# A row softmax on one Trainium2 core: the fourth chunk's load is split into rows 0 to 13 and rows 14 and 15

## The chip, the cores and the metric

The kernel runs on one core of a Trainium2 chip. The metric is the device time of one execution in microseconds (us), the median of several runs. One execution was also taken by the hardware profiler; all rows below come from it.

## The reference

```python
x: (16, 1024, 512) float32
x_scaled = x / 0.5
x_max = np.max(x_scaled, axis=-1, keepdims=True)
exp_x = np.exp(x_scaled - x_max)
out = exp_x / np.sum(exp_x, axis=-1, keepdims=True)
```

It is a softmax with temperature 0.5 over each of 16384 rows of 512 floats. 33.55 MB are read and 33.55 MB written.

## The kernel before

The 16384 rows are cut into 8 chunks (`C`), numbered from 0. A chunk gives each of the 128 partitions (`P`) 16 rows (`G`) that lie side by side in HBM, so one partition's share of a chunk is 32 KB in one piece, and a chunk is 4096 KB. Six buffers (`BUFS`) hold chunks; chunk 6 takes the buffer of chunk 0, and chunk 7 that of chunk 1, so their loads wait until those chunks have been stored.

**Loads.** `LOADS` lists, for each chunk, the row ranges that are loaded by a DMA each. Chunk 0 comes in two (rows 0 to 3, then 4 to 15), chunks 1 to 6 whole, chunk 7 without its last two rows (`LATE`). `load(c, queue)` issues them at L75. Chunk 0 goes on SyncE's queue. Chunks 1 and 3 go on ScalarE's queue at the very beginning; chunk 1 first waits until the first rows of chunk 0 have landed. The others are issued on SyncE's queue: 2, 4 and 5 at once, 6 after the store of chunk 0, 7 after the store of chunk 1. The last two rows of chunk 7 come on GpSimd's queue (`load_last_rows`, L111), in packets of 4 KB, after ScalarE has reached row 10 of chunk 5.

**Compute.** `BLOCKS` cuts the chunks into 11 blocks: chunk 0 into three, chunk 7 into two, the others whole. `shift(i)` finds a block's row maxima on VectorE (L92) and the bias of the exponential (L96). `exponentials` runs one instruction per row on ScalarE (L122), which also sums the row. `scale_vector` takes the reciprocal (L143) and multiplies most rows on VectorE (L145); `scale_scalar` multiplies the last few on ScalarE (L156). Everything works in place in the chunk's buffer. Only `shift` reads what a load has just brought: the maxima of a whole chunk wait for all of the chunk's DMAs.

**Stores.** Each chunk is stored whole, by one DMA on ScalarE's queue (L166), after its last block is scaled. So the queue of ScalarE carries, in this order, the loads of chunks 1 and 3 and then the eight stores. ScalarE issues them in the order of its own instructions.

**Order.** The schedule is written by hand (`tc.manual_schedule()`). The loop runs the exponentials of block i + 1, the scaling of block i, the maxima of block i + 2 and the store of block i. VectorE's order is therefore: scale a chunk, then the maxima two blocks on.

Of the kernel before, what the change touches and what calls it, by code (L numbers as in the profile page):

```python
# [1 line left out]

# [4 lines left out]


@with_exitstack
def kernel(  # L10
    ctx: ExitStack,
    tc: tile.TileContext,
    x: bass.AP,
    out: bass.AP,
):
    nc = tc.nc
    fp32 = mybir.dt.float32
    P = nc.NUM_PARTITIONS
    AX = mybir.AxisListType.X
    EXP = mybir.ActivationFunctionType.Exp  # L20
    COPY = mybir.ActivationFunctionType.Copy
    MAX = mybir.AluOpType.max

    D = x.shape[-1]
    xf = x.flatten_outer_dims()
    of = out.flatten_outer_dims()
    N = xf.shape[0]

    G = 16
    C = N // (P * G)
    assert C * P * G == N
    xr = xf.rearrange("(c p g) d -> c p g d", p=P, g=G)
    outr = of.rearrange("(c p g) d -> c p g d", p=P, g=G)
    WHOLE = [(0, G)]
    LATE = 2
    LOADS = [[(0, 4), (4, G)]] + [WHOLE] * 6 + [[(0, G - LATE)]]
    BLOCKS = [[(0, 4), (4, 8), (8, G)]] + [WHOLE] * 6 + [[(0, 8), (8, G)]]  # L40
    STORES = [WHOLE] * 8
    BMAX = 16
    BUFS = 6

    data = ctx.enter_context(tc.tile_pool(name="data", bufs=BUFS))
    stats = ctx.enter_context(tc.tile_pool(name="stats", bufs=6))

    ctx.enter_context(tc.manual_schedule())


    warm = stats.tile([P, 1], fp32, name="warm", bufs=1)
    nc.vector.memset(warm, 0.0)  # L52
    nc.scalar.activation(out=warm, in_=warm, func=EXP)  # L53

    chunks = {}
    blocks = [(c, lo, hi) for c in range(C) for lo, hi in BLOCKS[c]]
    n = len(blocks)
    biases, sums, recips = {}, {}, {}

    finished = []  # L60
    data_wait = mybir.DependencyInfo(
        mybir.DependencyClass.Sync, mybir.DependencyReason.DATA
    )
    for c in range(BUFS):
        chunks[c] = data.tile([P, G, D], fp32, name="xt")

    loaded = set()

    def load(c, queue):
        loaded.add(c)  # L70
        if c >= BUFS:
            chunks[c] = chunks[c - BUFS]
        xt = chunks[c]
        for lo, hi in LOADS[c]:
            part = queue.dma_start(out=xt[:, lo:hi, :], in_=xr[c][:, lo:hi, :])  # L75
            if c == 1:
                tc.add_manual_dep(
                    part.ins, finished[0], data_wait, reason="first rows come alone"
                )
            finished.append(part.ins.name)  # L80

    load(0, nc.sync)
    for c in (1, 3):
        load(c, nc.scalar)

    def shift(i):
        c, lo, hi = blocks[i]
        if c not in loaded:
            load(c, nc.sync)
        b = hi - lo  # L90
        negmax = stats.tile([P, BMAX], fp32, name="negmax")
        nc.vector.tensor_reduce(  # L92
            negmax[:, 0:b], chunks[c][:, lo:hi, :], axis=AX, op=MAX, negate=True
        )
        biases[i] = stats.tile([P, BMAX], fp32, name="bias")
        nc.vector.tensor_scalar_mul(biases[i][:, 0:b], negmax[:, 0:b], 2.0)  # L96

    def load_last_rows(signal):
        seen = stats.tile([P, 1], fp32, name="seen", bufs=1)
        copied = nc.gpsimd.tensor_copy(out=seen, in_=signal)  # L105
        finished.append(copied.ins.name)
        c = C - 1
        to = chunks[c - BUFS][:, G - LATE : G, :]
        of_ = xr[c][:, G - LATE : G, :]
        for p0, p1 in ((P - 2, P), (0, P - 2)):  # L110
            part = nc.gpsimd.dma_start(  # L111
                out=to[p0:p1], in_=of_[p0:p1], max_dma_last_dim=4 * D
            )
            finished.append(part.ins.name)

    def exponentials(i, rows):
        c, lo, hi = blocks[i]
        if i not in sums:
            sums[i] = stats.tile([P, BMAX], fp32, name="sums")
        for g in rows:  # L120
            row = chunks[c][:, lo + g, :]
            nc.scalar.activation(  # L122
                out=row,
                in_=row,
                func=EXP,
                bias=biases[i][:, g : g + 1],
                scale=2.0,
                accum_out=sums[i][:, g : g + 1],
            )
            if c == BUFS - 1 and g == 10:  # L130
                load_last_rows(sums[i][:, g : g + 1])


    def scalar_rows(i):
        c, lo, hi = blocks[i]
        return 4 if hi - lo == G else (hi - lo) // 8

    def scale_vector(i):
        c, lo, hi = blocks[i]
        b = hi - lo  # L140
        k = b - scalar_rows(i)
        recips[i] = stats.tile([P, BMAX], fp32, name="recip")
        nc.vector.reciprocal(recips[i][:, 0:b], sums[i][:, 0:b])  # L143
        rows = chunks[c][:, lo : lo + k, :]
        last = nc.vector.tensor_mul(  # L145
            rows, rows, recips[i][:, 0:k].unsqueeze(2).broadcast_to((P, k, D))
        )
        if i == n - 1:
            finished.append(last.ins.name)

    def scale_scalar(i):
        c, lo, hi = blocks[i]
        b = hi - lo
        for g in range(b - scalar_rows(i), b):
            row = chunks[c][:, lo + g, :]
            last = nc.scalar.activation(  # L156
                out=row, in_=row, func=COPY, scale=recips[i][:, g : g + 1]
            )
            if i == n - 1:
                finished.append(last.ins.name)  # L160

    def store(i):
        c, _, end = blocks[i]
        for lo, hi in STORES[c]:
            if hi == end:
                part = nc.scalar.dma_start(  # L166
                    out=outr[c][:, lo:hi, :], in_=chunks[c][:, lo:hi, :]
                )
                if c < C - 1:
                    finished.append(part.ins.name)  # L170

    shift(0)
    shift(1)

    def rows(i):
        c, lo, hi = blocks[i]
        cut = 6 if c == 1 else hi - lo
        return range(cut), range(cut, hi - lo)

    exponentials(0, rows(0)[0])  # L180
    for i in range(n):
        if i + 1 < n:
            exponentials(i + 1, rows(i + 1)[0])
        scale_vector(i)
        scale_scalar(i)
        if i + 2 < n:
            shift(i + 2)
        store(i)
        if i + 1 < n:
            exponentials(i + 1, rows(i + 1)[1])  # L190

    seen = nc.sync.nop()
    info = mybir.DependencyInfo(
        mybir.DependencyClass.Sync, mybir.DependencyReason.DATA
    )
    for name in finished:
        tc.add_manual_dep(seen.ins, name, info, reason="leaves one wait for the end")


# [1 line left out]
_INS = ['x']  # L201
_OUTS = [((16, 1024, 512), 'float32')]


# [23 lines left out]
```

## Time and profile before

| | |
|---|---|
| median of 3 runs | 161.92 us (161.68 to 162.12) |
| the profiled execution's own time | 161.71 us |
| its span, first to last instruction | 159.9 us |
| VectorE (DVE) busy | 128.3 us, 80% of the span |
| ScalarE (ACT) busy | 109.6 us, 69% of the span |
| bytes moved by DMA | 67.13 MB, 420 GB/s over the span |
| 4096 KB stores on ScalarE's queue | 8, median 20.9 us from issue to landing |

How to read it: the span leaves out some 1.8 us around the first and the last instruction. Busy time is counted for compute instructions alone; an instruction that issues a DMA or waits is not busy time. The lines of the page's second part cut the span into 40 slices of 4 us; the digit is the busy share in tenths. The 16 DMA engines of the core serve all queues; q10 in the profile is ScalarE's queue, q1 SyncE's and q0 GpSimd's. A packet is one contiguous piece, here one partition's share of a DMA, and is counted where it starts.

### The profile page before, as it was taken

The page shows a single profiled execution, that of the slowest core. Times are in us where ns is not written, and L with a number is a line of the kernel's source. Part 1 is how long each engine was busy: PE and PEld are TensorE (multiplying, and loading weights), DVE is VectorE, ACT ScalarE, POOL GpSimd, SP SyncE. Part 2 cuts the span into 40 slices and gives each one's busy share as a digit, 9 for nine tenths or more (in the row PEclk, how much of TensorE's full clock was granted, in tenths as well). Part 3 has the DMA queues.
Part 4 walks back from the last instruction along what each step waited for, and adds up shares of the span by engine and source line. Part 5 has one row for each costly group of instructions (what it writes and reads, how often), then busy time and mean ns, then how long its engine had stood idle before and what let it go on. Part 6 is the DMA issues. An engine that isn't in the chain of part 4 may idle for free.

```text
span 159.9 us, 422 instructions
## 1 busy us (share of the span) xinstructions
DVE 128.3 (80%) x45; ACT 109.6 (69%) x285; POOL 1.9 (1%) x7
## 2 busy tenths in 40 slices
DVE  0600599999999999999999999999999999955000
ACT  3070072924899999599959995999699899980000
POOL 0000000000000000000000000040000000000000
DMA  5999999999999999999999989898999999999994
GB/s 189 467 459 459 393 393 508 410 393 467 451 320 461 402 402 508 402 393 484 434 393 443 467 380 492 370 483 384 415 454 436 416 516 393 393 475 443 393 443 205
DMA packets 2642, 67.13 MB, mean 420 GB/s; under 512 B 336, under 2 KB 336, under 8 KB 464
## 3 DMA queue, kind: packets, MB, share of 16 engines
q10 hardware_dynamic: 1440, 41.94, 60.8%
q1 hardware_dynamic: 1008, 24.64, 36.5%
q0 software_dynamic: 192, 0.52, 0.8%
q14 instruction: 2, 0.02, 0.0%
HBM read 33.55 MB, written 33.55 MB: 420 GB/s over the span
## 4 chain that ended last, share of the span: by engine, by line
DVE 66%; ACT 10%; DMA 10%; issue 4%; SPq 0%
DVE negmax L92 39%; DVE xt L145 25%; ACT xt L122 10%; DMA xt<-in_x_dram 10%; DVE recip L143 1%; DVE bias L96 1%; SPq L75 0%
## 5 line engine op out<-in xcount | busy, mean ns | idle before, releaser
L122 ACT ACTIVATE xt<-xt,bias 128x512 f32<-128x512 f32 x128 | 90.4, 708 | 32.9 <-DVE bias L96 31.6
L92 DVE TENSOR_REDUCE negmax<-xt 128x16 f32<-128x8192 f32 (+2 forms) x11 | 69.9, 6353 | 14.2 <-DMA xt<-in_x_dram 14.2
L145 DVE TENSOR_TENSOR xt<-xt,recip 128x6144 f32<-128x6144 f32 (+2 forms) x11 | 55.6, 5056 | 0.4
L122 ACT ACTIVATION_READ_ACCUMULATOR xt<-xt,bias 128x1 f32 x128 | 23.9, 187 | 0.0
L156 ACT ACTIVATE xt<-xt,recip 128x512 f32<-128x512 f32 x27 | 17.3, 706 | 0.0
L143 DVE RECIPROCAL recip<-sums 128x16 f32<-128x16 f32 (+2 forms) x11 | 2.4, 220 | 2.1 <-ACT xt L122 2.1
L96 DVE TENSOR_SCALAR bias<-negmax 128x16 f32<-128x16 f32 (+2 forms) x11 | 1.9, 173 | 0.4
L53 ACT ACT_TABLE_LOAD x1 | 1.3, 1283 | 0.7 <-PEq L212 0.7
L111 POOL DMA_DIRECT2D xt<-in_x_dram x2 | 1.5, 744 | 0.5 <-issue 0.5
L105 POOL COPY seen<-sums 128x1 f32<-128x1 f32 x1 | 0.2, 186 | 105.2 <-ACT xt L122 105.2
L52 DVE MEMSET warm<- 128x1 f32 x1 | 0.1, 59 | 0.8 <-PEq L212 0.8
L53 ACT ACTIVATE warm<-warm 128x1 f32<-128x1 f32 x1 | 0.2, 203 | 0.0
L212 POOL MEMSET const-bfloat16-1.0<- 128x1 bf16 x1 | 0.1, 96 | 0.0
L212 POOL MEMSET const-uint8-127<- 128x1 uint8 x1 | 0.1, 96 | 0.0
L212 POOL MEMSET const-float32-0.0<- 128x1 f32 x1 | 0.1, 93 | 0.2 <-issue 0.2
L212 POOL MEMSET const-float32-1.0<- 128x1 f32 x1 | 0.1, 93 | 0.0
## 6 DMA issues: line engine op xcount, KB each, us to landing
out_dram<-xt ACTq DMA_DIRECT2D x8, 4096.0 KB, 20.9
xt<-in_x_dram SPq DMA_DIRECT2D x4, 4096.0 KB, 45.3
xt<-in_x_dram ACTq DMA_DIRECT2D x2, 4096.0 KB, 31.4
xt<-in_x_dram SPq DMA_DIRECT2D x1, 3584.0 KB, 25.3
xt<-in_x_dram SPq DMA_DIRECT2D x1, 3072.0 KB, 16.4
xt<-in_x_dram SPq DMA_DIRECT2D x1, 1024.0 KB, 4.7
xt<-in_x_dram POOLq DMA_DIRECT2D x1, 504.0 KB, 19.2
xt<-in_x_dram POOLq DMA_DIRECT2D x1, 8.0 KB, 8.6
```

What stands on the lines that cost most here:

```text
L52: nc.vector.memset(warm, 0.0)
L53: nc.scalar.activation(out=warm, in_=warm, func=EXP)
L92: nc.vector.tensor_reduce(negmax[:, 0:b], chunks[c][:, lo:hi, :], axis=AX, op=MAX, negate=True)
L96: nc.vector.tensor_scalar_mul(biases[i][:, 0:b], negmax[:, 0:b], 2.0)
L105: copied = nc.gpsimd.tensor_copy(out=seen, in_=signal)
L111: part = nc.gpsimd.dma_start(out=to[p0:p1], in_=of_[p0:p1], max_dma_last_dim=4 * D)
L122: nc.scalar.activation(out=row, in_=row, func=EXP, bias=biases[i][:, g : g + 1], scale=2.0, accum_out=sums[i][:, g : g + 1],)
L143: nc.vector.reciprocal(recips[i][:, 0:b], sums[i][:, 0:b])
L145: last = nc.vector.tensor_mul(rows, rows, recips[i][:, 0:k].unsqueeze(2).broadcast_to((P, k, D)))
L156: last = nc.scalar.activation(out=row, in_=row, func=COPY, scale=recips[i][:, g : g + 1])
L212: nc = _bacc.Bacc("TRN2", target_bir_lowering=False, num_devices=1)
```

## The change

`LOADS` gets a cut in its fourth entry, chunk 3. Its rows 0 to 13 of every partition (28 KB) are loaded by one DMA, and rows 14 and 15 (4 KB) by a second, both on ScalarE's queue, one behind the other, in the place where the one DMA of 32 KB per partition stood. Nothing else is edited: the same loop in `load` issues them, and the maxima of chunk 3 read both parts.

```diff
     WHOLE = [(0, G)]
     LATE = 2
-    LOADS = [[(0, 4), (4, G)]] + [WHOLE] * 6 + [[(0, G - LATE)]]
+    TAIL = 2
+    LOADS = [[(0, 4), (4, G)]] + [WHOLE] * 2 + [[(0, G - TAIL), (G - TAIL, G)]] + [WHOLE] * 3 + [[(0, G - LATE)]]
     BLOCKS = [[(0, 4), (4, 8), (8, G)]] + [WHOLE] * 6 + [[(0, 8), (8, G)]]
```

## The prediction

> **What bounds the kernel now.** I read the page first: VectorE is busy 80% of the span and ScalarE 69%, and the chain of waits puts two thirds of the span on VectorE, so VectorE looks like the bound. The page's slices of the DMA engines say otherwise:
>
> ```profile
> DMA  5999999999999999999999989898999999999994
> GB/s 189 467 459 459 393 393 508 410 393 467 451 320 461 402 402 508 402 393 484 434 393 443 467 380 492 370 483 384 415 454 436 416 516 393 393 475 443 393 443 205
> ...
> q10 hardware_dynamic: 1440, 41.94, 60.8%
> q1 hardware_dynamic: 1008, 24.64, 36.5%
> q0 software_dynamic: 192, 0.52, 0.8%
> ```
>
> The 16 DMA engines are full from the second slice to the last but one. q10 carries 41.94 MB, which is what ScalarE's queue issues (two loads and eight stores of 4096 KB); q1 carries SyncE's loads, q0 GpSimd's 512 KB. A whole load or store is 128 rows of 32 KB, 8 packets for each of 16 engines. What one costs I read in a stretch late in the run, where q10 works alone, in the DMA view (columns: packets, MB, share of 16 engines):
>
> ```profile
> q10 hardware_dynamic: 155, 4.55, 105.5%
> ```
>
> That is 140 to 150 us: 1.055 x 10 us x 16 engines = 168.8 us for 4.55 MB = 139 packets of 32 KB (the other 16 are the 4-byte packets that close a DMA), 1.214 us each. The whole job is 67.1 MB / 16 = 4.19 MB per engine = 128 such packets = 155.4 us. The span is 159.9, so all that is not plain transfer (start, end, disturbance) is 4.5 us.
>
> One disturbance is visible: slice 12 (44 to 48 us) moves 320 GB/s, the lowest of all but the first and last. Neighbouring slices swing because a packet counts at its start, so I took a window cut on packet starts, 44.6 to 47.8 us:
>
> ```profile
> DMA packets 48, 1.05 MB, mean 328 GB/s; under 512 B 16, under 2 KB 16, under 8 KB 16
> ...
> q1 hardware_dynamic: 32, 1.05, 99.1%
> q10 hardware_dynamic: 16, 0.00, 0.3%
> ```
>
> Two load packets of 32 KB per engine fill 99.1% of 3.2 us x 16 engines: 1.586 us each instead of 1.214. The loss is 2 x 0.37 = 0.75 us on every engine. q10 shows only closing packets: here the fourth chunk's load ends on ScalarE's queue and the first store behind it begins. The change sits exactly there. The landings, from the same view by single issues:
>
> ```profile
> xt<-in_x_dram ACTq DMA_DIRECT2D x1, 4096.0 KB, 41.0
> out_dram<-xt ACTq DMA_DIRECT2D x1, 4096.0 KB, 23.8
> ```
>
> The fourth chunk (second of ScalarE's two loads, issued at 5.84) lands at 46.9; the first store, issued at 43.23, lands at 67.1. Last, the timeline, for who needs the chunk and how much room there is at the end:
>
> ```profile
> 57.71 8.68 DVE L92 TENSOR_REDUCE negmax<-xt 128x16 f32<-128x8192 f32 x1
> ...
> 127.16 0.34 ACTq L166 DMA_DIRECT2D out_dram<-xt  x1
> ```
>
> 57.71 is the fourth chunk's maximum, with VectorE busy without a gap before it: the chunk has lain ready for 10.8 us. 127.16 is the store of the sixth chunk, and it is the tightest point between the compute and the DMA: the store before it was issued at 111.61 and lands 18.3 us later, at 129.9. A DMA on an idle queue has some 2.3 us outside its data (the very first: 4.7 us to landing, of which 8 packets of 8 KB, a quarter of 1.214 each, are 2.4). So the store's data could follow without a gap if it were issued as late as 129.9 - 2.3 = 127.6: compute may come at least 0.5 us late before the DMA engines run dry. The first DMA had slow start-up packets, so the room may be nearer 0.9.
>
> **The change part by part.**
>
> *One more DMA instruction on ScalarE.* The two loads there take 0.86 us from 5.42, 0.4 each; the third would end near 6.7. Behind it in ScalarE's order stands only the first exponential, which starts at 7.95 because its bias comes then. Cost nothing, covered by 1.2 us; uncovered it would be 0.4. No other queue is passed. The maximum at L92 waits for two completions instead of one; a wait already met costs a semaphore instruction (17 to 28 ns for SyncE's), and VectorE has 0.5 us to give.
>
> *Packets.* 8 packets per engine of 32 KB become 8 of 28 KB and 8 of 4 KB, and one more closing packet. The trace has 4 KB packets, those of GpSimd's last rows on q0: 0.8% of 159.9 x 16 = 20.5 us for 128 of them, 0.16 each (0.15 to 0.17 by the rounding), against 1.214 / 8 = 0.152. The excess is 8 x 0.008 = 0.07 us per engine, 0 to 0.15, and it is fully exposed since the engines have no idle time: +0.07.
>
> *Order.* Between 37.4 and 44.7 us the queues q1 and q10 get 49 and 48 packets: one each in turn, whatever the size. So the first 14 rows land 8 x 0.152 = 1.2 us earlier than the chunk does now: 46.9 less 1.2, and less the part of the stall that came before the landing (some 0.3), about 45.4. Then each 4 KB packet waits for one 32 KB load packet: 8 x (1.214 + 0.16) = 11.0 us, so rows 14 and 15 land at about 56.4. VectorE asks at 57.71: 1.3 us of room. If the stall falls before that landing, 0.6 remain. So the landing goes from 10.8 us of room to about one, but stays hidden, and VectorE's own chain does not move.
>
> *What follows on the queues.* The first store stands behind the small packets: its data start near 57.5 instead of 47.9. The loads on q1 take the turns that it leaves: chunks five and six land earlier. The bytes moved by a given time are the same, the engines being full. With some 4 packets of chunk six left to alternate with, the store's 8 packets end near 57.5 + 12 x 1.214 = 72. SyncE's load of the seventh chunk, which waits for that store, goes out 5 us later than now (67.15); even with the 28.6 us it takes now it lands at 101, and its maximum starts at 104.37. Until it goes out, q10 alone keeps the engines full, as it does at 140 us, since the second store was issued at 64.95. From then on the order is that of before.
>
> *The stall.* Its 0.75 us are the only thing large enough to be measured, and the trace has it once. It stays if it belongs to the first write to HBM: this store is the first, all 16 engines lose the same, and no other end of a load or start of a store shows it. It goes if it comes from a whole 32 KB load packet giving way to a store on the same queue, since the queue now ends in 4 KB packets. Ends: 0.75 gained, to 0.75 lost (stalled twice, the small packets included). I take no change: the first write is still there, with the same two queues active, and a stall of full engines is paid wherever it falls. A gain of 0.75 would move the store's start at 127.6 that much earlier, which the room of 0.5 to 0.9 just allows.
>
> [...]
>
> **The sum.** 161.71 (the profiled execution) + 0.07 + 0 = 161.8; it stands 0.21 below the median of the runs, 161.92, so I forecast **162.0**, no change. About 0.3%, 0.5 us, is what a measurement here can tell from none.
>
> **The rivals.**
>
> *The stall goes (faster).* 161.92 + 0.07 - 0.75 = 161.25, 0.4% faster. For it: the stall is at the very place that is edited, and lies on load packets, before the store's own, so it may be a matter of handing over. Against: nothing in the trace shows a handover from small packets to a store.
>
> *The last two rows come late (slower).* If small packets miss turns, each miss costs 1.214 us. The first is covered by the 1.3 us before 57.71; VectorE late by more than the 0.5 to 0.9 at the sixth chunk's store delays the end one for one. So it decides from a landing of about 58.4: at three missed turns (60.0, 2.3 late, less 0.7) it is 163.6; if all eight missed one, 66.1, and 169.7. For it: only about one microsecond of cover is left. Against: the 4 KB packets on q0 and the equal counts on q1 and q10.
>
> *The split does nothing to the order* (the small pieces pass together): the store starts as now, and the time is 162.0 again; it counts with the forecast.
>
> **How the numbers follow.** No change 0.38 (161.5 to 162.4); the stall goes 0.35 (160.9 to 161.4, since a part of it may stay or a skew of the engines' ends may add); slower 0.27, of which about 0.15 is the late rows and 0.12 a stall that grows (up to 162.7). The range 160.9 to 163.2 leaves out most of the late rows' case and a little below, under 2 in 10; the likeliest case's own range is 161.5 to 162.4. Faster 0.35, same 0.38, slower 0.27.
>
> **What would show it.** Right: a 4096 KB load in two issues on ScalarE's queue, the 512 KB one landing near 56; no idle time of VectorE before the maximum at 57.7; the first store landing near 72 and the seventh chunk's load issued just after; and somewhere between 44 and 60 us a stretch in which 32 KB packets take well over 1.214. Wrong: no such stretch (then 161.25), VectorE waiting on a DMA at 57.7 (then slower), or slices below full between 60 and 156 us.

## The result, and the profile after

The changed kernel takes 162.43 us (median of 22 runs, 162.28 to 163.17) against 162.04 us (22 runs, 161.66 to 162.46) for the kernel before in the same rounds. The ratio is 1.0030, 95% interval 1.0022 to 1.0038. The forecast was no change at 162.0; the kernel became 0.39 us slower by the medians and 0.50 by the means, which lies on the bound of 0.3% that the forecast drew, and 162.43 stands just above the likeliest case's own range (161.5 to 162.4). The profiled execution took 162.39 us, with a span of 160.3 (before: 161.71 and 159.9).

Each run lists its time and its span (to 0.1 us), and the difference is what the span leaves out. Over the 22 executions of the changed kernel it is 2.13 us on average (2.09 to 2.18). For the kernel before it is 1.78 (1.73 to 1.84, the 80 executions made beside the experiments below). So some 0.35 us of the loss lie outside the span, where the views of the profile show nothing, and 0.05 (by the medians) to 0.15 (by the means) inside it.

First the page after: the 40 slices and the queues.

```profile
DMA  5999999898999989999999999898999999999993
GB/s 194 460 458 458 393 393 500 383 474 376 491 427 449 361 335 507 401 393 507 409 393 491 427 393 483 368 491 378 443 415 435 456 458 409 409 491 409 393 491 155
...
q10 hardware_dynamic: 1584, 41.94, 60.7%
q1 hardware_dynamic: 1008, 24.64, 36.5%
```

Slice 12 has risen from 320 to 427 GB/s, and the dip now stands in slices 14 and 15 (361 and 335): the stall has moved by some 10 us and not gone. q10 has 144 packets more for the same bytes: 128 pieces and 16 closing packets. The single issues of ScalarE's queue, from the DMA view (KB each, us from issue to landing):

```profile
xt<-in_x_dram ACTq DMA_DIRECT2D x1, 3584.0 KB, 39.6
...
xt<-in_x_dram ACTq DMA_DIRECT2D x1, 512.0 KB, 50.9
...
out_dram<-xt ACTq DMA_DIRECT2D x1, 4096.0 KB, 29.3
```

Issued at 5.86, 6.33 and 43.24, they land at 45.5 (rows 0 to 13), 57.2 (rows 14 and 15) and 72.5 (the first store). Now the timeline of the two engines that these could hold up:

```profile
5.44 1.36 ACTq L76 DMA_DIRECT2D xt<-in_x_dram  x3
7.96 0.72 ACT L123 ACTIVATE xt<-xt,bias 128x512 f32<-128x512 f32 x1 [5.72 <-DVE bias L97]
...
57.72 8.68 DVE L93 TENSOR_REDUCE negmax<-xt 128x16 f32<-128x8192 f32 x1
```

The third issue ends at 6.80, before the first exponential, which starts at 7.96 as before (7.95). The fourth chunk's maximum starts at 57.72, with no idle time in brackets: the last rows came half a microsecond ahead. The waits agree, since VectorE's whole wait for loads is that of before, 14.2 us in 2 waits:

```profile
DVE negmax L93 <- DMA xt<-in_x_dram: 14.2, 2, 9.7
```

Last, the stall, in two windows of the DMA view cut on packet starts: 46.3 to 54.2 us, while the small pieces take turns, and 54.2 to 57.65, where the queue goes over to the store.

```profile
q1 hardware_dynamic: 97, 2.65, 78.4%
q10 hardware_dynamic: 96, 0.39, 12.2%
...
q1 hardware_dynamic: 32, 1.05, 95.4%
q10 hardware_dynamic: 32, 0.07, 5.0%
```

In the first, q10's 96 pieces of 4 KB take 0.122 x 7.9 x 16 / 96 = 0.161 us each, and q1's 2.65 MB = 81 load packets 0.784 x 7.9 x 16 / 81 = 1.223. In the second, 32 load packets take 0.954 x 3.45 x 16 / 32 = 1.646 us each in place of 1.214: 0.86 us lost per engine, where the kernel before lost 0.74 (0.991 x 3.2 x 16 / 32 = 1.586 us each; the prediction has 0.75). Below, "the loss" of a window is always worked out so.

### The profile page after: what moved, and what is told of

The parts are those of the page before. It is cut to its first block, busy times and chain, and to the rows that moved or that the text cites. A ratio compares the mean times of both kernels' runs of the same rounds, so it can differ in the third digit from the quotient of the medians.

```text
span 160.3 us, 424 instructions
## 1 busy us (share of the span) xinstructions
DVE 128.3 (80%) x45; ACT 109.6 (68%) x285; POOL 1.9 (1%) x7
## 2 busy tenths in 40 slices
DMA packets 2786, 67.13 MB, mean 419 GB/s; under 512 B 352, under 2 KB 352, under 8 KB 608
## 4 chain that ended last, share of the span: by engine, by line
DVE 66%; ACT 10%; DMA 10%; issue 4%; SPq 0%
DVE negmax L93 39%; DVE xt L146 25%; ACT xt L123 10%; DMA xt<-in_x_dram 10%; DVE recip L144 1%; DVE bias L97 1%; SPq L76 0%
## 5 line engine op out<-in xcount | busy, mean ns | idle before, releaser
L93 DVE TENSOR_REDUCE negmax<-xt 128x16 f32<-128x8192 f32 (+2 forms) x11 | 69.9, 6352 | 14.2 <-DMA xt<-in_x_dram 14.2
L123 ACT ACTIVATION_READ_ACCUMULATOR xt<-xt,bias 128x1 f32 x128 | 23.8, 186 | 0.0
```

The lines of the kernel that those rows point to most:

```text
L93: nc.vector.tensor_reduce(negmax[:, 0:b], chunks[c][:, lo:hi, :], axis=AX, op=MAX, negate=True)
L123: nc.scalar.activation(out=row, in_=row, func=EXP, bias=biases[i][:, g : g + 1], scale=2.0, accum_out=sums[i][:, g : g + 1],)
```

## The experiments

The theory: nothing but the DMA engines sets the time, and the change costs by what it does to them: the packets themselves, and a stall that goes with the first store. Rivals: the stall is a handover of a load to a store on one queue; the 4 KB packets or the extra DMA are the cost; the late first store is the cost. The theory looks inside the span alone; what the span leaves out is taken up with the last experiment.

**Is it chance?** Both kernels were profiled a second time.

> The kernel before once more, for a second profile: how far do the stall and the spread of the engines' ends differ from one execution to the next? If the stall is a property of the kernel: 0.75 us again at 44.6 to 47.8 us, 328 GB/s there. If it is chance: somewhere else, or none.

> The changed kernel once more, for a second profile. If the larger stall (0.9 us in place of 0.75) is a property of the later first store: 0.85 to 0.95 again, at 54 to 58 us. If it is chance: between 0.6 and 1.0 with no order against the kernel before.

The kernel before (161.74 us) again, 44.6 to 47.85 us; then the changed one (162.30 us), 54.2 to 57.65 and 84 to 88 us:

```profile
q1 hardware_dynamic: 32, 1.05, 97.1%
```

```profile
q1 hardware_dynamic: 32, 1.05, 92.0%
...
q1 hardware_dynamic: 33, 1.08, 68.1%
```

The losses: 0.73 us before (0.74 in the first profile), 0.75 after (0.86 in the first). So the stall is a property of the kernel: both profiles of each have it in the same place. Its being larger after the change is not: it has no order between these profiles. In the second profile of the changed kernel another disturbance came near 84 to 88 us, where its 33 load packets take 1.321 us, a loss of 0.22; the first profile of it has none there (36 packets in 68.2% of the same window, 1.212 us).

**Is the stall the first write to HBM?** A copy of 64 KB, planned over all 16 DMA engines, or one row of 512 bytes is written to the output at the start; the last store, which writes over it, waits for it.

```diff
     load(0, nc.sync)
+    early = nc.scalar.dma_start(out=outr[C - 1][:, 0, 0:128], in_=xr[C - 1][:, 0, 0:128])
     # the second kernel: [0:1, 0, 0:128]
```

> The kernel before, plus one small copy at the very start on ScalarE's queue: 128 pieces of 512 bytes from the input to the last chunk's place in the output, spread over all 16 DMA engines and written over by the last store. Theory A (the stall belongs to the first write to HBM): the 0.75 us stall near 44.7 to 48 us is gone, 32 KB load packets there take 1.21 us; the median falls by up to 0.7, to about 161.3, or stays near 162.0 if the stall is only paid earlier. Theory B (the stall belongs to a load handing over to a store on the same queue): the stall near 45 us stays at 1.55 to 1.6 us per packet, and the median is 162.0 to 162.2.

> As the first experiment, but the early copy is one piece of 512 bytes, so one DMA engine writes to HBM early. Theory A, the first write of each engine: 15 engines still stall near 45 us and one does not; median 162.0. Theory A, the first write of the core as a whole: all 16 are free of the stall; median about 161.3. Theory B: all 16 stall as before; median 162.0.

Measured: 162.60 us (ratio 1.0032, 1.0013 to 1.0050) and 162.22 (1.0016, 0.9998 to 1.0034). The DMA view of the first, 44.8 to 48.15 us:

```profile
q1 hardware_dynamic: 32, 1.05, 95.5%
```

The loss is 0.77 us with the early copy of 64 KB, and 0.82 in the second kernel (32 load packets in 95.4% of 44.6 to 48 us). The second kernel is not the one-engine case that was meant: from 4.4 to 5.4 us its q10 shows 32 packets, 16 pieces (512 / 16 = 32 bytes each) and 16 closing ones, so the row was cut in 16.

```profile
q10 hardware_dynamic: 32, 0.00, 1.8%
```

It isn't the first write as such. The first kernel's time is also above both expectations; the span holds most of that, and why is not known. What a small copy at the start does not settle is whether the first large store matters.

**Is it the store, the end of the load, or the queue?** The first store was issued on GpSimd's queue, and, in another kernel, on ScalarE's but only just ahead of the second store.

```diff
-                part = nc.scalar.dma_start(
+                # for c == 0 alone, with max_dma_last_dim=G * D:
+                part = nc.gpsimd.dma_start(
```

```diff
-        store(i)
+        if blocks[i][0] == 1:
+            store(i - 1)
+        if blocks[i][0] != 0:
+            store(i)
```

> The kernel before, with the store of chunk 0 issued on GpSimd's queue in place of ScalarE's. The first store then follows no load on its own queue, and ScalarE's queue is empty from the end of chunk 3's load until the second store. Theory B1 (a store right behind a load on one queue): no packet above 1.25 us between 43 and 50 us, and, the 0.75 us being the largest disturbance, a median of 161.3 to 161.6. Theory B2 (the first large store beside loads, on whatever queue): load packets of 1.5 us or more still appear within 5 us of the issue at 43.2, 0.75 us per engine in sum, and the median is 161.9 to 162.5.

> The kernel before, with the store of chunk 0 issued just ahead of the store of chunk 1, near 65 us in place of 43.2. ScalarE's queue ends its loads near 46 us with nothing behind them. If the stall belongs to the end of the load: slow load packets at 44 to 48 us as before. If it belongs to the first large store: none there, and 0.7 us of slow packets, or none if no load is left to slow, just after 65 us. The time itself, near 168 us, is that of the DMA engines running dry before the stores (SyncE's loads of chunks 4 and 5 end near 59 us), and says nothing about the stall.

With GpSimd's queue, 45.9 to 51 us in the DMA view:

```profile
q1 hardware_dynamic: 64, 2.10, 103.9%
q0 software_dynamic: 32, 0.26, 12.1%
```

The load packets take 1.325 us, a loss of 0.44 per engine, as the store's first pieces start: smaller than expected under B2, but there, with no load ahead of the store on its queue. The time, 165.73 us (1.0222, 1.0199 to 1.0245), missed both figures: GpSimd's queue cut the store into 8 KB pieces (0.26 MB in 32), and it landed 37.5 us after its issue at 43.6, where ScalarE's had taken 23.8. That these pieces take one turn each is the author's explanation, which no view shows. Chunk 6's load, which waits for it, went out at 81.3, and the engines were 62% busy from 80 to 82 us and 33% from 150 to 153.

In the other kernel the store went out at 59.85 us and the time was 163.59 in one run, not 168, since it was issued before the loads ended. The DMA view at the end of chunk 3's load (44.6 to 47.8 us), then where ScalarE's queue goes from the second store to the third (84.0 to 88.5):

```profile
q1 hardware_dynamic: 47, 1.54, 111.6%
...
q1 hardware_dynamic: 29, 0.95, 69.2%
```

At the end of the load, 1.216 us a packet: no stall at all. Near 86 us, 1.718, a loss of 0.91 between two stores, where the kernel before has none (38 load packets in 64.0% of the same window, 1.213 us). The same trace has two more such places, in which the slow packets are those of stores: 60 to 62 us, where the first store begins with one load packet left, and 74.4 to 76.2, just before the seventh chunk's load (issued at 71.99) moves its first data:

```profile
q10 hardware_dynamic: 18, 0.59, 87.2%
...
q10 hardware_dynamic: 20, 0.66, 112.9%
```

That is 1.55 and 1.63 us a packet, losses of 0.38 and 0.51. So the end of a load does not make the stall, the first store is not its only occasion, and it does not fall on load packets alone.

**What does a late first store cost, with no split?** The store of chunk 0 was put inside the exponentials, after row 12 of chunk 1 or row 7 of chunk 2.

```diff
+            if c == 2 and g == 7:    # the other kernel: c == 1 and g == 12
+                store(2)
...
-        store(i)
+        if i != 2:
+            store(i)
```

> The kernel before, with the store of chunk 0 issued inside the exponentials of chunk 1, near 48.6 us in place of 43.2, when ScalarE's queue has emptied. No DMA is added and SyncE's loads keep the engines full meanwhile. If the stall needs a store waiting behind the load's last packets: no packets above 1.25 us at 44 to 50 us, and with the 0.75 us saved 161.2 to 161.5, faster than both kernels. If the stall belongs to the first store beside loads, whenever it starts: 0.6 to 0.9 us of excess at about 50 to 53 us, and 161.9 to 162.2.

> As the experiment with the store at 48.6 us, but issued near 56.7 us, so that its data start about when they do in the changed kernel (57.7), with no second DMA for chunk 3 and no 4 KB packets. If the later first store by itself costs the changed kernel its 0.39 us: 162.3 to 162.5. If the split costs it: 161.9 to 162.1, or 161.2 to 161.5 if the stall goes as well.

The first missed its mark. ScalarE issued the store at 44.11 us, 4.5 us ahead of the place that was expected, so chunk 3's load was still on the queue. It measured 161.90 us (0.9983, 0.9971 to 0.9996), with a loss of 0.83 between 44.6 and 48.0 in its profile (an execution of 162.28 us): it does not answer the question. The second was issued at 52.82, 5 us after chunk 3 had landed (47.6), on an empty queue, and its data began near 57.6, as in the changed kernel. It measured 162.34 us (1.0023, 1.0006 to 1.0040). The DMA view, 54 to 57.5 us:

```profile
q1 hardware_dynamic: 32, 1.05, 92.4%
```

1.617 us a packet, a loss of 0.81, on an empty queue: the handover theory falls. With chunk 3 in one DMA and no small packet the late store alone comes within 0.07% of the changed kernel's ratio, but not by the same way: what its span leaves out is 1.78 us, as before, and all of its loss lies inside the span.

**What do the packets cost, with no late store?** Three cuts. Chunk 3 in rows 0 to 7 and 8 to 15 (as late, no 4 KB pieces); chunk 5 in 14 and 2 rows on SyncE's queue (4 KB pieces, first store untouched); and the changed kernel's cut with rows 14 and 15 on SyncE's queue, behind chunk 2.

```diff
-    TAIL = 2
+    TAIL = 8
```

```diff
-    LOADS = [[(0, 4), (4, G)]] + [WHOLE] * 6 + [[(0, G - LATE)]]
+    LOADS = [[(0, 4), (4, G)]] + [WHOLE] * 4 + [[(0, G - 2), (G - 2, G)]] + [WHOLE] + [[(0, G - LATE)]]
```

```diff
+    LOADS = [[(0, 4), (4, G)]] + [WHOLE] * 2 + [[(0, G - 2)]] + [WHOLE] * 3 + [[(0, G - LATE)]]
...
+        if c == 2:
+            part = nc.sync.dma_start(
+                out=chunks[3][:, G - 2 : G, :], in_=xr[3][:, G - 2 : G, :]
+            )
```

> The changed kernel, but cut into rows 0 to 7 and 8 to 15: two DMAs of 16 KB pieces in place of 28 KB and 4 KB. The chunk takes the same 16 turns against SyncE's 32 KB packets, so it lands near 56 to 57.5 us and the first store is as late as in the changed kernel, but there are no 4 KB packets. If the changed kernel's 0.39 us come from the late first store (a larger stall and engines out of step): 162.3 to 162.5. If they come from the 4 KB packets: 162.0 to 162.1.

> The kernel before, with chunk 5 (SyncE's queue) cut into rows 0 to 13 and 14 to 15 in place of none; ScalarE's queue is as before. The same number of 4 KB packets as in the changed kernel, with no change to the first store. If the small packets by themselves cost: 162.1 (0.07 by the 0.16 us of one) to 162.4 (all of the 0.39). If the cost comes from the later first store: 162.0 to 162.1, with the stall near 45 us unchanged.

> The same two DMAs for chunk 3 as in the changed kernel, rows 0 to 13 on ScalarE's queue, but rows 14 and 15 on SyncE's, behind chunk 2's load. The small packets then stand ahead of chunk 4 and not ahead of the first store, which starts near 46 us as in the kernel before. If the later first store is what costs the changed kernel its time: 162.0 to 162.15, the 4 KB packets giving 0.06 to 0.08 us. If the split itself does (two waits, a DMA more, small packets): 162.3 to 162.5 again. Slow load packets of 0.6 to 0.9 us in sum are expected between 43 and 49 us in either case.

| | median | ratio, interval |
|---|---|---|
| halves | 162.47 us | 1.0022, 1.0009 to 1.0034 |
| chunk 5 cut | 162.48 us | 1.0032, 1.0014 to 1.0050 |
| rows 14, 15 on SyncE's queue | 162.33 us | 1.0014, 1.0000 to 1.0027 |

The halves fall where the late store was expected, without 4 KB pieces; but they too have a DMA more, and their stall is smaller than before the change (32 load packets in 86.0% of 54.5 to 58 us, a loss of 0.58). The chunk 5 cut costs as much with an early store, above the 162.1 that the packets alone would give. In its profile the first stall is unchanged (32 load packets in 99.1% of 44.6 to 47.8 us, 0.74), but from 80 to 86 us, where the small pieces end, q1's 2.18 MB take 88.2% of the window: 84.7 us of engine time, where 1.214 per 32 KB makes 80.8, a loss of 0.24. The last cut puts small pieces ahead of chunk 4 and leaves the store where it was; its 162.33 falls where the split itself was expected to cost. In its DMA view, 44.5 to 47.9 us:

```profile
q1 hardware_dynamic: 32, 1.05, 97.0%
```

1.649 us a packet, 0.87 lost. It costs 162.33 - 162.12 = 0.21 us, though neither the first store nor its landing (67.1 us) has moved. So a late store is not needed for a loss of this size, and by the halves small packets are not either; what all three cuts have in common is a DMA more.

**Does one DMA more cost in itself?** Chunk 3 by two DMAs of 64 partitions each, all rows.

```diff
+            half = slice(0, P // 2)    # the second DMA: slice(P // 2, P)
-            part = queue.dma_start(out=xt[:, lo:hi, :], in_=xr[c][:, lo:hi, :])
+            part = queue.dma_start(out=xt[half, lo:hi, :], in_=xr[c][half, lo:hi, :])
```

> The kernel before, with chunk 3 loaded by two DMAs of 64 partitions each, all 16 rows: one DMA more, as in the changed kernel, but the same 32 KB packets, and the first store only one turn (1.2 us) later. If a DMA more costs in itself: 162.3 to 162.5. If the 4 KB packets or the ten microseconds of delay cost: 161.9 to 162.1, with the stall at 45 to 49 us near 0.75.

It measured 173.89 us (1.0724, 1.0709 to 1.0740). The median does not answer the question, since the kernel does something else as well, told at the end. What the spans leave out does. The table has the mean time less span of all executions of a kernel, and its mean span against that of the kernel before in the same rounds (95% interval; for the changed kernel against the 80 executions):

| | executions | time less span | span against before |
|---|---|---|---|
| the kernel before | 80 | 1.78 us (1.73 to 1.84) | |
| first store late, in two kernels | 11, 11 | 1.77, 1.78 | -0.17 (-0.35 to 0.01), +0.34 (0.08 to 0.60) |
| early writes, in two kernels | 12, 12 | 1.85, 1.86 | +0.44 (0.19 to 0.69), +0.22 (-0.02 to 0.46) |
| first store on GpSimd's queue | 5 | 1.94 (1.83 to 2.03) | +3.56 |
| chunk 5 cut | 12 | 2.05 (1.99 to 2.09) | +0.24 (0.03 to 0.45) |
| rows 14, 15 on SyncE's queue | 11 | 2.05 (2.01 to 2.10) | -0.05 (-0.24 to 0.14) |
| changed kernel | 22 | 2.13 (2.09 to 2.18) | +0.09 (-0.03 to 0.21) |
| halves | 12 | 2.13 (2.08 to 2.17) | +0.06 (-0.05 to 0.17) |
| by partition | 4 | 2.14 (2.11 to 2.18) | +11.46 |

In all five kernels that cut a load in two, 0.27 us (on SyncE's queue) to 0.35 (on ScalarE's) are added outside the span, with pieces of 4 to 32 KB and with the first store early or late; issuing the first store later on ScalarE's queue adds none, a small copy 0.07, and the first store on GpSimd's queue, with no DMA more, 0.15. So a second DMA for a load did cost in itself here, and in the changed kernel, the halves and the cut with rows 14 and 15 on SyncE's queue that is most or all of the loss. What takes this time, and whether at the start or at the end, no view of the profile shows; it stays open.

## Why the prediction was right

*The bound.* Right inside the span: VectorE's rows are the same to 0.02 us, and what changed there is on the DMA engines.

*ScalarE's third issue* was foretold to end near 6.7 and ended at 6.80, covered inside the span; it is the term that was mis-sized, below. *Order*: rows 0 to 13 at 45.4, measured 45.5; rows 14 and 15 at 56.4, with 0.7 us less room if the stall fell ahead of that landing: it did, and they came at 57.2, 0.5 us before VectorE asked. The first store's landing near 72 came at 72.5, and the seventh chunk's load went out at 72.70 and landed 23.5 us later, at 96.2, long before 104.4. The rival with late rows needed 1.2 us more.

*One turn each.* That the small pieces pass together, as in the last rival, loses against the trace: the eight of each engine took a turn each, with a load packet between (81 load packets to 96 pieces in the window above), and landed at 57.2, 11.7 us after rows 0 to 13.

*The stall stays.* Right, and for the likeliest case decisive, but partly by luck: the first reason given, the first write to HBM, was wrong, since with 64 KB written early the loss was still 0.77 us. What the runs show is load packets that slowed down from 1.214 us where the first store started beside them: to between 1.505 (the halves) and 1.649 (rows 14 and 15 on SyncE's queue) behind a load on ScalarE's queue, to 1.617 on an empty queue, to 1.325 with the store on GpSimd's. In the kernel with the first store just ahead of the second, packets of stores slowed down too (1.55 and 1.63), once just before a load's data began. Why they do is open; so is why some starts cost 0.9 us (near 86 us in that kernel) and the same ones in other kernels nothing.

*The mis-sized term.* The sum has +0.07, for 0.39 measured. The step that failed is "Cost nothing" for the DMA instruction more: it is hidden inside the span, but what the span leaves out, which the sum took over unchanged in its 161.71, grew by 0.35 us. Inside the span the sum was about right: +0.07 foretold, 0.05 to 0.15 found. The packets gave what was said, 8 x (0.161 - 0.152) = 0.07. The load packets between the small ones took 1.223 us, those that alternate between 37.4 and 44.7 us before the change 0.512 x 7.3 x 16 / 49 = 1.220 (51.2% of that window for 49), so next to nothing is lost there. The stall is 0.74 and 0.73 us in the two profiles before, 0.86 and 0.75 in the two after, and 0.58 in the halves with a store as late: its part is not told apart from chance. Nor is that of the late first store: alone it added 0.34 us to the span (0.08 to 0.60), but the changed kernel and the halves, whose store is as late, show 0.09 and 0.06. That the forecast of no change held although this term was missing is owed to its size, 0.2% of the time.

## What to carry to other kernels

Where the DMA engines are full, count the turns: here a load packet of 1.223 us took its turn between each two of the eight 4 KB pieces of an engine, and the first store, which stood behind them on the queue, began its data at 57.7 us in place of 47.9 and landed at 72.5 in place of 67.1. The move cost little, 0.05 to 0.15 us inside the span, since the landings had cover; and it gained nothing either, with the same 67.13 MB to move. When a change is forecast near nothing in such a kernel, forecast the losses that the trace before shows once, and price a DMA more by itself: here 0.27 to 0.35 us outside the span for a load cut in two. Before a difference of a few tenths is looked for among packets, compare the time less the span of all runs; here that number told kernels apart that their medians did not.

## What the runs showed of the hardware

A load cut by partitions did not behave like one cut by rows: 173.89 us, against 162.47 for the halves. In the kernel with two DMAs of 64 partitions the page's slices (4.3 us each here) from 26 to 60 us fall to 236 to 353 GB/s. The DMA view from 30 to 57 us (columns as before):

```profile
q10 hardware_dynamic: 127, 3.64, 57.5%
q1 hardware_dynamic: 123, 3.51, 42.0%
```

q10's 3.64 MB are 111 packets of 32 KB at 0.575 x 27 x 16 / 111 = 2.24 us, and the 107 of SyncE's whole chunks on q1 take 1.70, against 1.214. In this window alone that is (111 x 1.02 + 107 x 0.48) / 16 = 10.3 us per engine, most of the 11.8 that the kernel lost. The second half landed 54.6 us after its issue, at 61.1, and VectorE waited 2.3 us for it (20.3 for loads in all, 14.2 before). The 2.24 us are 1.84 times the 1.214; why, no view of the runs shows.

Also not expected: in the two kernels with the store among the rows, ScalarE issued the DMA ahead of activations that stand before it in its program: at 44.11 and 52.82 us, while the last row before it ended only near 48.1 and 56.9, some 4 us later. So a transfer that was placed between these rows to delay it was delayed by less than their durations.
